# Gathering the rows of several experts in one product, behind a row norm applied before the split

## The chip, the core and the metric

The kernel runs on one core of a Trainium2 chip. The metric is the device time of one execution in microseconds (us). Engines are named as the profile names them: PE (TensorE, with PEld its weight loads), ACT (ScalarE), DVE (VectorE), POOL (GpSimd) and SP (SyncE, here the queue that issues the loads).

## What is computed

Two layers of a decoder trunk over 256 tokens of 1024 features, all in float32. Layer 0 has differential attention and a state-space scan, then a dense SwiGLU. Layer 1 has two other attention kinds, then a routed mixture of experts, with which this change deals:

```python
def rms_norm(t, gain):
    return t * rsqrt(mean(t * t, axis=-1) + 1e-6) * gain

def swiglu(h, w_gate, w_up, w_down):
    return (silu(h @ w_gate) * (h @ w_up)) @ w_down

h = rms_norm(x, od_norm_ffn)
logits = h @ router                           # 256 x 8
top_val, top_idx = top_k(logits, 2)
gates = sum(one_hot(top_idx, 8) * softmax(top_val)[..., None], axis=1)
for e in range(8):                            # w_gate, w_up: 1024 x 2816
    out = out + gates[:, e:e + 1] * swiglu(h, w_gate[e], w_up[e], w_down[e])
x = x + out
```

Each expert's three matrices are 34.6 MB together, and all eight are read in every execution.

## The kernel before

**Precision.** Products that need float32 are made of three faster ones: a value is split into a high and a low part (`wh` on ACT, `wl` on DVE for weights, `fh`/`fl` or `xnh`/`xnl` for rows), and `mm3` (L496 to L500) multiplies high by high, low by high and high by low.

**Routing** (L1305 to L1358). In two halves of 128 tokens the rows `x3` are transposed, multiplied by the router (products of 8 columns), and split unnormed into `xnh` and `xnl`; the row scale `rows` (`block_rstd`, L560) is worked out after the choice `m`. Products on `m` count the positions of the tokens in each expert. The experts are put in the order of their number of tokens; `ids` holds that order. The first four are the large ones (up to 128 tokens each), the last four the small ones (up to 64).

**Gathering.** An expert's tokens are brought together by a product with a one-hot matrix (`one_hots` L1415, `gather` L1427): for each of 8 blocks of 128 features four products, `xnh` and `xnl` by two halves of tokens. A pass takes the large expert of number p (128 columns) and its small partner (64 columns) at once, 192 columns; large rows are split on the way out, small ones copied to `xs`. Since the gathered rows aren't normed, `slot_scale` (L1440) gathers the row scales as well (products of one column), and Silu and the product of gate and up take them as operands. The first large expert is gathered before the loop (128 columns), its small partner in chunks 0 to 2 of that expert (64 columns), and each next pair in chunks 3 to 10 of the large expert before, one block of features in each.

**The loop.** An expert's 2816 inner features are 11 chunks of 256. A chunk of any expert needs three loads of 1 MiB: two of gate and up, one of down. A large chunk splits its weights and uses three products; a small chunk streams the raw weights by its rows. The order is fixed: LAG = 3 large chunks alone, then pairs of one large and one small chunk, then 3 small chunks alone. The down product of a chunk is put behind the gate and up products of the next one. Behind the last chunk of an expert its rows are scattered back by another one-hot product.

**The loads** all go through SP's queue in the order in which they are used (`Stream`, L673). A load needs a place: RAW = 4 raw buffers, and buffers of the earlier layers that have become free (`xres`, `xg0` up to unit XG = 12, `xg1`, `more`, `fl`). The addresses of all experts but the first two in line depend on `ids`, so SP reads `ids` (L1539) ahead of the first such load. Until the loop begins, work is recorded and ordered by a list scheduler (its lines are L312, DMAs L428); in the loop instructions stand as written (L317, DMAs L424).

If an expert had more than 128 tokens, a branch behind the loop would do its work in another way; it isn't taken here.

Of the kernel before, what the change touches and what calls it, by code (L numbers as in the profile page):

```python
# [19 lines left out]
P = 128  # L20
# [37 lines left out]
EXPLN = "natural_log_exp_and_others"  # L58
SILU = "silu_and_others"
# [316 lines left out]
def kernel(ctx: ExitStack, tc: tile.TileContext, a, out: bass.AP):  # L376
# [133 lines left out]
    def bc(ap, shape):  # L510
        return ap.to_broadcast(shape)
# [243 lines left out]
    def ff_act(gu, scales, act=None):  # L755
        hs = []
        for b in range(len(gu)):
            si = tw(256)
            (act or tact)(si, gu[b][:, 0:256], AF.Silu, scale=scales[b])
            hh = tw(256)  # L760
            V.scalar_tensor_tensor(hh, gu[b][:, 256:512], scales[b], si, op0=OP.mult, op1=OP.mult)
            hs.append(hh)
        return hs

# [553 lines left out]
    rows, slots = mo([P, 2], "rows"), mo([P, 8], "slots")  # L1318
# [93 lines left out]
    def one_hot(t, pos):  # L1412
        V.tensor_scalar(t, iota, pos, None, op0=OP.is_equal)

    def one_hots(p):  # L1415

        t = tw(dt=F32R).rearrange("p (b e s) -> p b e s", b=2, e=2)
        for b in range(2):
            one_hot(t[:, b, 0, :], (poso if p else posm)[:, b, p:p + 1])
            V.tensor_scalar(t[:, b, 1, :].rearrange("p (i s) -> p i s", i=2), bc(iota[:, None, 0:HALFP], [P, 2, HALFP]),  # L1420
                            poso[:, b, BIG + p:BIG + p + 1], None, op0=OP.is_equal)
        return t

    oh = {0: one_hots(0)}


    def gather(k, ohs, xb=None, xs=None):  # L1427

        lo, hi = 0 if xb else P, P + HALFP if xs is not None else P
        o = pa()[:, lo:hi]  # L1430
        for i, src in enumerate((xnh, xnl)):
            for b in range(2):
                mmx(o, src[:, b, k * P:(k + 1) * P], ohs(b)[:, lo:hi], i + b == 0, i + b == 2)
        gain = k2("gf1k", k, k + 1)
        if xb:
            split_gain(xb[0][:, k], xb[1][:, k], o[:, 0:P], gain)
        if xs is not None:
            S.activation(xs[:, k], o[:, P - lo:hi - lo], AF.Copy, scale=gain)

    def slot_scale(dst, ohs):  # L1440

        sp, n = pa(), ohs.shape[2]
        for e in range(n):
            for b in range(2):
                mmx(sp[:, e:e + 1], ohs[:, b, e, :].bitcast(F32), rows[:, b:b + 1], b == 0, b == 1)
        V.tensor_copy(dst, sp[:, 0:n])

    def oht_of(oh0, oh1):
        tp = pa()
# [24 lines left out]
                    dma(ov[:, b, cs], acc[:, b, cs])  # L1474
        rec.late = 0

    def large_tile(p):
        t = mo([P, 2, 8, P], "xg0", F32R) if p % 2 else gtile([P, 2, 8, P], F32R, "fh")
        return t[:, 0], t[:, 1]

    def small_tile():
        return rec.tile(mo.pool, [P, 8, HALFP], F32, "mxs", 2, name="xs")


    def sm_gu(xs, gu, u):
# [6 lines left out]
                    wv[:, :, i * P:(i + 1) * P], k == 0, k == 7)  # L1492
        st.done()

    def sm_act(gu, scale):
        si, hh = tw(P), tw(P)
        tact(si, gu[:, 0:P], AF.Silu, scale=scale)
        V.scalar_tensor_tensor(hh, gu[:, P:256], scale, si, op0=OP.mult, op1=OP.mult)
        return hh

    def sm_tr(hh):
# [49 lines left out]
    xb, xs = {0: large_tile(0)}, {}  # L1551
    for k in range(8):
        gather(k, lambda b: oh[0][:, b].rearrange("p e s -> p (e s)"), xb[0])
    rec.late = AFTER
    slot_scale(slots[:, 0:2], oh[0])
    rec.late = 0
    rec.flush([x3, oh[0], *xb[0], *st.tiles()])
    rec.on = False
    at.close()
    ov = out.rearrange("(b p) d -> p b d", p=P)  # L1560
    ys, ohts, hs, pend = {}, {}, {}, None
    N = len(items)
    for i in range(N + 1):
# [3 lines left out]
        if it:  # L1567
            sm, p, c = it
            gu = pa()
            xsp = [(xb[p][0], xb[p][1])] if not sm else xs[p]  # L1570
            sm_gu(xsp, gu, 0) if sm else ff_gu(st, xsp, [gu], 0, False)
        if was:
            t = sm_tr(hs[was]) if was[0] else ff_tr(hs[was])
        st.ahead(HL if alone or it[0] else HL - 1)
        if it:
            sm_gu(xsp, gu, 1) if sm else ff_gu(st, xsp, [gu], 1, False)
            e = 2 * p + sm
            hs[it] = sm_act(gu, slots[:, e:e + 1]) if sm else ff_act([gu], [slots[:, e:e + 1]])
        if alone or it[0]:
            st.ahead(HL)  # L1580
        if was:
# [12 lines left out]
        if not it:  # L1594
            continue
        if c == 1:
            ohts[sm] = oht_of(*(oh[p][:, b, int(sm), :] for b in range(2)))
        if sm:
            continue
        both = lambda b, q: oh[q][:, b].rearrange("p e s -> p (e s)")  # L1600
# [12 lines left out]
    scatter(*pend)  # L1613
    man.close()

# [2 lines left out]
    with tc.If(many > P):  # L1618
        with tc.For_i(0, 8, 1) as ei:
            col = small([P, 2, 2], "col")  # L1620
            V.tensor_copy(col[:, 0, :], posx[:, :, bass.ds(ei, 1)].rearrange("p b e -> p (b e)"))
            V.tensor_copy(col[:, 1, :], gate[:, :, bass.ds(ei, 1)].rearrange("p b e -> p (b e)"))
            ohx = tw(256, dt=F32R).rearrange("p (b s) -> p b s", b=2)
            for b in range(2):
                one_hot(ohx[:, b, :], col[:, 0, b:b + 1])
            xo = large_tile(1)
            for k in range(8):
                gather(k, lambda b: ohx[:, b, :], xo)
            slot_scale(slots[:, 0:1], ohx[:, :, None, :])
            to = oht_of(ohx[:, 0, :], ohx[:, 1, :])  # L1630
            yo = [[pa(), pa()]]
            st = Stream([a["moe"][bass.ds(ei * (3 * FC) + j, 1)].rearrange("u p c -> p (u c)") for j in range(3 * FC)])
            for c in range(FC):
                gu = [pa()]
                ff_gu(st, [xo], gu, 0)
                ff_gu(st, [xo], gu, 1)
                ff_dn(st, ff_tr(ff_act(gu, [slots[:, 0:1]], S.activation)), yo, c == 0, c == FC - 1)
            scatter(to, y_split(yo[0]), lambda b: col[:, 1, b:b + 1], x3)
        dma(ov, x3)
    mo.close()  # L1640


# [151 lines left out]
```

## Time and profile before

| what | value |
|---|---|
| median of 3 runs | 1177.9 us (1177.27 to 1180.31) |
| profiled execution | 1181.26 us, span 1179.5 us |
| PE busy | 1152.2 us, 98% of the span |
| PEld, DVE, ACT busy | 843.8, 718.6, 602.6 us |
| loaded from HBM | 345.95 MB, mean 294 GB/s over the span |
| share of PE in the chain that ended last | 83% (DMA 8%, DVE 4%, ACT 3%) |

The chain that ended last is followed back from the last instruction to whatever released each one. The expert loop runs from about 486 us to the end; before it lie the two layers' attention and the dense SwiGLU. In the windows below, a stretch of time is cut out of the span and each engine's busy time in it is given with its number of instructions. The timeline rows give start and length of one group of like instructions; a length reaches to the end of the last one, so neighbours overlap, and the distance of two starts tells what one took.

### The profile page before, as it was taken

The page shows a single profiled execution, that of the slowest core. Times are in us where ns is not written, and L with a number is a line of the kernel's source. Part 1 is how long each engine was busy: PE and PEld are TensorE (multiplying, and loading weights), DVE is VectorE, ACT ScalarE, POOL GpSimd, SP SyncE. Part 2 cuts the span into 40 slices and gives each one's busy share as a digit, 9 for nine tenths or more (in the row PEclk, how much of TensorE's full clock was granted, in tenths as well). Part 3 has the DMA queues.
Part 4 walks back from the last instruction along what each step waited for, and adds up shares of the span by engine and source line. Part 5 has one row for each costly group of instructions (what it writes and reads, how often), then busy time and mean ns, then how long its engine had stood idle before and what let it go on. Part 6 is the DMA issues. An engine that isn't in the chain of part 4 may idle for free.

```text
span 1179.5 us, 16563 instructions
## 1 busy us (share of the span) xinstructions
PE 1152.2 (98%) x6171; PEld 843.8 (72%) x6171; DVE 718.6 (61%) x1179; ACT 602.6 (51%) x1015; POOL 28.6 (2%) x59
## 2 busy tenths in 40 slices
PE   6999999999999999999999999999999999999997
PEld 6887888888777878876666666666666666666663
DVE  5999945444389765784555665556565546565542
ACT  5767743444388565564445444445445554444431
POOL 1040000000300000000000000000000000000000
PEclk9999999999999999799999999999999999999999
DMA  9443455556353513378999999999999999999994
GB/s 353 153 177 108 144 213 179 181 181 225 107 175 131 208 55 134 134 291 356 387 393 417 399 411 394 405 423 421 380 415 411 408 395 402 418 409 422 416 413 164
DMA packets 52069, 348.13 MB, mean 295 GB/s; under 512 B 5904, under 2 KB 6032, under 8 KB 11536
## 3 DMA queue, kind: packets, MB, share of 16 engines
q1 hardware_dynamic: 51984, 347.02, 74.6%
q8 instruction: 50, 0.82, 0.3%
q14 instruction: 35, 0.29, 0.1%
HBM read 345.95 MB, written 1.05 MB: 294 GB/s over the span
## 4 chain that ended last, share of the span: by engine, by line
PE 83%; DMA 8%; DVE 4%; ACT 3%; issue 2%; SPq 0%; DVEq 0%; ACTq 0%
PE ps L317 21%; PE ps L498 17%; PE ps L500 17%; PE ps L499 17%; PE ps L312 11%; DMA raw<-in_moe_dram 3%; ACT wh L317 2%; DVE wl L317 2%; DMA fl<-in_moe_dram 2%; DMA xg<-in_moe_dram 1%; DMA more<-in_moe_dram 1%; ACT tw L312 1%; DMA raw<-in_w_dram 1%; DMA xres<-in_moe_dram 1%; DVE wl L312 0%
## 5 line engine op out<-in xcount | busy, mean ns | idle before, releaser
L317 DVE TENSOR_TENSOR wl<-raw,wh 128x2048 fp32r<-128x2048 f32 x90 | 206.3, 2293 | 160.7 <-ACT wh L317 160.7
L317 ACT ACTIVATE wh<-raw 128x2048 fp32r<-128x2048 f32 x90 | 172.0, 1911 | 118.1 <-DMA raw<-in_moe_dram 63.9
L498 PE MATMUL ps<-wh,fh 128*128 128x512 f32 (+2 forms) x544 | 221.5, 407 | 0.0
L499 PE MATMUL ps<-wl,fh 128*128 128x512 f32 (+2 forms) x544 | 211.3, 388 | 0.0
L500 PE MATMUL ps<-wh,fl 128*128 128x512 f32 (+2 forms) x368 | 142.2, 387 | 0.0
L317 ACT ACTIVATE tw<-ps 128x128 f32<-128x128 f32 (+2 forms) x114 | 43.3, 388 | 180.0 <-PE ps L317 178.0
L498 PEld LDWEIGHTS ps<-wh,fh 128*128 128x128 f32 x544 | 103.2, 190 | 20.6 <-ACT tw L312 0.3
L498 PE MATMUL ps<-wh,tw 128*128 128x512 f32 (+1 forms) x276 | 113.9, 413 | 1.7 <-ACT tw L317 1.0
L499 PEld LDWEIGHTS ps<-wl,fh 128*128 128x128 f32 x544 | 103.1, 190 | 17.3
L500 PE MATMUL ps<-wh,tw 128*128 128x512 f32 (+1 forms) x276 | 109.0, 395 | 0.0
L499 PE MATMUL ps<-wl,tw 128*128 128x512 f32 (+1 forms) x276 | 108.9, 395 | 0.0
L312 DVE TENSOR_TENSOR wl<-raw,wh 128x512 fp32r<-128x512 f32 (+1 forms) x149 | 98.9, 679 | 2.9 <-ACT wh L312 2.8
L317 DVE TENSOR_TENSOR tw<-ps,tw 128x256 fp32r<-128x256 f32 (+1 forms) x70 | 35.9, 521 | 91.8 <-ACT tw L317 91.6
L312 ACT ACTIVATE wh<-raw 128x512 fp32r<-128x512 f32 (+1 forms) x135 | 77.7, 623 | 19.7 <-PE ps L500 16.1
L317 PE MATMUL ps<-raw,xs 128*64 128x256 f32 x720 | 87.2, 384 | 0.0
L500 PEld LDWEIGHTS ps<-wh,fl 128*128 128x128 f32 x368 | 69.1, 188 | 14.8 <-DVE fl L312 0.7
L498 PEld LDWEIGHTS ps<-wh,tw 128*128 128x128 f32 x276 | 51.8, 188 | 28.1 <-issue 15.4
L498 PE MATMUL ps<-wh,xg 128*128 128x512 f32 x176 | 71.0, 403 | 0.0
L500 PE MATMUL ps<-wh,fh 128*128 128x512 f32 x176 | 69.8, 396 | 0.0
L317 PEld LDWEIGHTS ps<-raw,xs 128*64 128x64 f32 x720 | 48.4, 136 | 29.8 <-issue 8.5
L500 PE MATMUL ps<-wh,xg 128*128 128x512 f32 x176 | 69.3, 394 | 0.0
L499 PE MATMUL ps<-wl,xg 128*128 128x512 f32 x176 | 68.7, 390 | 0.0
(295 smaller groups left out, 1807.3 us busy)
## 6 DMA issues: line engine op xcount, KB each, us to landing
raw<-in_moe_dram SPq DMA_DIRECT2D x131, 1024.0 KB, 9.3
xg<-in_moe_dram SPq DMA_DIRECT2D x33, 1024.0 KB, 8.9
xres<-in_moe_dram SPq DMA_DIRECT2D x33, 1024.0 KB, 8.3
more<-in_moe_dram SPq DMA_DIRECT2D x32, 1024.0 KB, 8.7
fl<-in_moe_dram SPq DMA_DIRECT2D x32, 1024.0 KB, 8.6
raw<-in_ffn_dram SPq DMA_DIRECT2D x30, 1024.0 KB, 4.8
raw<-in_w_dram SPq DMA_DIRECT2D x23, 1024.0 KB, 5.2
raw<-in_ffn_dram SPq DMA_DIRECT2D x12, 256.0 KB, 3.8
```

Of the source, the lines that this page charges most:

```text
L312: return (self.name, self.cost(fn, args, kw), lambda: real(*args, **kw))
L317: return getattr(self.eng, fn)(*args, **kw)
L498: nc.tensor.matmul(ps, xh, wh, start=start, stop=False)
L499: nc.tensor.matmul(ps, xh, wl, start=False, stop=False)
L500: nc.tensor.matmul(ps, xl, wh, start=False, stop=stop)
```

## The change

- The row scale is worked out ahead of the split, and `split_gain` puts it into `xnh` and `xnl`. The gathered rows are normed, `slot_scale` and `slots` go, and Silu and the product of gate and up lose their scale operands.
- `one_hots(lo, n, width)` makes one-hot matrices of several experts. All four small experts are gathered in one pass (4 x 64 columns) in chunks 0 to 3 of the first large expert, two blocks of features in each. Large experts 1 and 2 are gathered together (2 x 128 columns) in chunks 6 to 9 of the first, and large expert 3 (128 columns) in chunks 2 to 5 of the second. ACT copies them unsplit to a tile in the place `xg0`.
- `large_split` splits an expert's rows into the one tile `fh` behind the gate and up products of the last chunk of the expert before it (one ACT copy, one DVE subtraction, 128x1024).
- RAW 4 to 5, XG 12 to 14, LAG 3 to 4.
- `WARM` = 8 products of 512 columns, whose result is not used, stand between the router products and the products on `m`.

```diff
-RAW = 4
+RAW = 5
...
-XG = 12
+XG = 14
...
-LAG = 3
+LAG = 4
+WARM = 8
...
+            if scales:
...
+            else:
+                (act or tact)(si, gu[b][:, 0:256], AF.Silu)
+                V.tensor_tensor(hh, gu[b][:, 256:512], si, OP.mult)
...
         rx3 = rows[:, b:b + 1]
+        block_rstd(x3, b, rx3)
...
-            flex(xnh[:, b, cs], x3[:, b, cs])
-            V.tensor_tensor(xnl[:, b, cs], x3[:, b, cs], xnh[:, b, cs].bitcast(F32), OP.subtract)
+            split_gain(xnh[:, b, cs], xnl[:, b, cs], x3[:, b, cs], rx3)
...
-        block_rstd(x3, b, rx3)
...
+    idle = pa()
+    rec.late = AFTER
+    for i in range(WARM):
+        mmx(idle, u3r[:, 0:P], xnh[:, 1, 0:512], True, True)
+    rec.late = 0
...
+    def one_hots(lo, n, width=P):
+
+        t = tw(2 * n * width, dt=F32R).rearrange("p (b e s) -> p b e s", b=2, e=n)
         for b in range(2):
...
+            V.tensor_tensor(t[:, b], bc(iota[:, None, 0:width], [P, n, width]),
+                            bc(poso[:, b, lo:lo + n, None], [P, n, width]), OP.is_equal)
         return t
...
+    def gather_all(k, oh, dst):
+
+        n, w = oh.shape[2], oh.shape[3]
+        o, gain = gather(k, lambda b: oh[:, b].rearrange("p e s -> p (e s)"), n * w)
+        S.activation(dst[:, :, k], o.rearrange("p (e s) -> p e s", e=n), AF.Copy, scale=gain)
...
+    def large_split(src):
+        x = large_tile()
+        S.activation(x[0], src, AF.Copy)
+        V.tensor_tensor(x[1], src, x[0].bitcast(F32), OP.subtract)
+        return x
...
-    slot_scale(slots[:, 0:2], oh[0])
...
+            if not sm and c == FC - 1 and p < BIG - 1:
+                xb = large_split(xl[:, p % 2])
...
         if p == 0 and c < LAG:
-            if c == 0:
-                xs[0] = small_tile()
-            for k in range(c * 3, min(8, c * 3 + 3)):
-                gather(k, lambda b: both(b, 0), None, xs[0])
-        if p < BIG - 1 and c == 2:
-            oh[p + 1] = one_hots(p + 1)
-        if p < BIG - 1 and c >= LAG:
-            if c == LAG:
-                xb[p + 1], xs[p + 1] = large_tile(p + 1), small_tile()
-                slot_scale(slots[:, 2 * p + 2:2 * p + 4], oh[p + 1])
-            gather(c - LAG, lambda b: both(b, p + 1), xb[p + 1], xs[p + 1])
+            for k in range(2 * c, 2 * c + 2):
+                gather_all(k, oh_s, xs)
+        if p == 0 and LAG + 2 <= c < LAG + 6:
+            if c == LAG + 2:
+                xl, oh_l = mo([P, 2, 8, P], "xg0"), one_hots(1, 2)
+            for k in range(2 * (c - LAG - 2), 2 * (c - LAG - 1)):
+                gather_all(k, oh_l, xl)
+        if p == 1 and 2 <= c < 6:
+            if c == 2:
+                oh_l = one_hots(3, 1)
+            for k in range(2 * c - 4, 2 * c - 2):
+                gather_all(k, oh_l, xl[:, 0:1])
```

On PE, between the router products (`tw` 128x8) and the first gather products (`tw,xnh` 128x128), before:

```order
L312 MATMUL ps<-cp,xres 128x128 x16
L312 MATMUL ps<-tw 128x8 x16
L312 MATMUL ps<-m,tw 128x8
L312 MATMUL ps<-m,tw 128x16
L312 MATMUL ps<-m,tw 128x8 x2
L312 MATMUL ps<-tw,xnh 128x128 x5
```

and after (`xnh,tw` 128x512 are the spare products):

```order
L313 MATMUL ps<-cp,xres 128x128 x4
L313 MATMUL ps<-tw 128x8 x12
L313 MATMUL ps<-xnh,tw 128x512 x8
L313 MATMUL ps<-m,tw 128x8
L313 MATMUL ps<-m,tw 128x16
L313 MATMUL ps<-m,tw 128x8 x2
L313 MATMUL ps<-tw,xnh 128x128 x5
```

The eight spare products stand where PE had nothing between the last router product and the first on `m`.

On SP, the expert loads ahead of the reading of `ids`, before:

```order
L428 DMA xg_3349<-in_moe_dram 128x2048
L428 DMA raw<-in_moe_dram 128x2048 x4
L428 DMA xres<-in_moe_dram 128x2048
L428 DMA raw<-in_moe_dram 128x2048 x2
L428 DMA xg_3356<-in_moe_dram 128x2048
L428 DMA more<-in_moe_dram 128x2048
L428 DMA fl<-in_moe_dram 128x2048
L1539 TENSOR_LOAD ids
```

and after:

```order
L429 DMA raw<-in_moe_dram 128x2048
L429 DMA xg_3350<-in_moe_dram 128x2048
L429 DMA raw<-in_moe_dram 128x2048 x4
L429 DMA xres<-in_moe_dram 128x2048
L429 DMA raw<-in_moe_dram 128x2048 x2
L429 DMA xg_3357<-in_moe_dram 128x2048
L429 DMA more<-in_moe_dram 128x2048
L429 DMA fl<-in_moe_dram 128x2048
L429 DMA raw<-in_moe_dram 128x2048 x2
L1558 TENSOR_LOAD ids
```

Eleven loads stand ahead of `ids` before, fourteen after.

On PE, chunk 3 of the third large expert with the small chunk behind it, before:

```order
L500 MATMUL ps<-wh,fh 128x512
L317 MATMUL ps<-fl,tw 64x512 x4
L317 MATMUL ps<-rows,tw 128x1 x4
L317 MATMUL ps<-tw,xnh 128x192 x2
L317 MATMUL ps<-tw,xnl 128x192 x2
L317 MATMUL ps<-xg_7522,xs 64x256 x8
L317 MATMUL ps<-cp,tw 128x128 x2
L317 MATMUL ps<-raw,xs 64x256 x8
```

and after:

```order
L501 MATMUL ps<-wh,fh 128x512
L318 MATMUL ps<-more,tw 64x512 x4
L318 MATMUL ps<-fl,xs 64x256 x8
L318 MATMUL ps<-cp,tw 128x128 x2
L318 MATMUL ps<-raw,xs 64x256 x8
```

The slot products (128x1) and gather products (128x192) are gone from this chunk.

## Rows read from the trace of the kernel before

**Rows 1.** The page: busy time of engines, and the clock's slices
```profile
PE 1152.2 (98%) x6171; PEld 843.8 (72%) x6171; DVE 718.6 (61%) x1179; ACT 602.6 (51%) x1015; POOL 28.6 (2%) x59
...
PEclk9999999999999999799999999999999999999999
```

**Rows 2.** Windows: start:end length, busy PE PEld DVE ACT POOL, clock, DMA share, GB/s
```profile
689.11:859.91 170.80, 170.80 (x932) 113.59 (x930) 99.31 (x93) 83.01 (x97) 0.00 (x0) 1.00 0.99 406
859.91:1030.75 170.84, 170.84 (x931) 113.51 (x930) 98.15 (x89) 83.81 (x98) 0.00 (x0) 1.00 0.99 407
```

**Rows 3.** Windows of single pairs, the first with a gather, the others without
```profile
722.53:737.76 15.23, 15.23 (x85) 10.07 (x84) 7.93 (x9) 7.59 (x9) 0.00 (x0) 1.00 1.01 424
...
1062.31:1076.78 14.47, 14.47 (x82) 9.65 (x80) 7.40 (x7) 6.84 (x7) 0.00 (x0) 1.00 1.01 423
...
1105.69:1121.39 15.70, 14.51 (x81) 9.64 (x80) 7.95 (x6) 7.02 (x8) 0.00 (x0) 1.00 1.01 421
1121.39:1136.28 14.89, 14.53 (x81) 9.63 (x80) 7.96 (x6) 6.57 (x7) 0.00 (x0) 1.00 1.00 398
```

**Rows 4.** Timeline of PE around one gather: start, length, line, operation, shapes, count
```profile
727.34 0.47 PE L317 MATMUL ps<-tw,xnh 128*128 128x192 f32 x2
...
727.96 1.95 PE L317 MATMUL ps<-raw,xs 128*64 128x256 f32 x16
```

**Rows 5.** Timeline of PE at narrow products; groups from 486 us on (busy, mean ns)
```profile
493.65 0.30 PE L317 MATMUL ps<-tw,xnh 128*128 128x64 f32 x2
...
494.90 0.48 PE L498 MATMUL ps<-wh,fh 128*128 128x512 f32 x1
...
363.89 0.28 PE L498 MATMUL ps<-wh,tw 128*128 128x256 f32 x1
...
364.60 0.40 PE L498 MATMUL ps<-wh,fh 128*128 128x512 f32 x1
...
L317 PE MATMUL ps<-tw,xnh 128*128 128x192 f32 x48 | 11.1, 314 | 0.0
...
L317 PE MATMUL ps<-rows,tw 128*128 128x1 f32 x24 | 3.1, 248 | 0.0
```

**Rows 6.** The routing stretch: its window, then timeline of PE and of DVE
```profile
473.21:490.28 17.07, 14.48 (x59) 13.46 (x59) 13.13 (x73) 6.18 (x15) 0.00 (x0) 0.50 0.33 112
...
469.98 4.08 PE L312 MATMUL ps<-tw 128*128 128x8 f32 x32
475.83 1.02 PE L312 MATMUL ps<-m,tw 128*128 128x8 f32 x4 [1.78 <-DVE m L312]
477.66 1.30 PE L312 MATMUL ps<-tw,xnh 128*128 128x128 f32 x5 [0.81 <-DVE rank L312]
...
484.52 1.81 PE L312 MATMUL ps<-rows,tw 128*128 128x1 f32 x8
486.19 0.77 PE L498 MATMUL ps<-wh,fh 128*128 128x512 f32 x1
...
490.18 0.45 PE L498 MATMUL ps<-wh,fh 128*128 128x512 f32 x1
...
478.23 0.68 DVE L312 TENSOR_TENSOR wl<-raw,wh 128x512 fp32r<-128x512 f32 x1
```

**Rows 7.** Waits (total, times, longest) of ACT, SP, PE; timeline of ACT; page's groups
```profile
ACT wh L317 <- DMA raw<-in_moe_dram: 63.9, 24, 5.4
...
SPq L1539 <- DVE ids L312: 11.9, 1, 11.9
...
PE ps L317 <- DVE tw L317: 2.8, 6, 1.2
...
1106.30 1.91 ACT L317 ACTIVATE wh<-more 128x2048 fp32r<-128x2048 f32 x1 [5.57 <-DMA more<-in_moe_dram]
...
L317 DVE TENSOR_TENSOR wl<-raw,wh 128x2048 fp32r<-128x2048 f32 x90 | 206.3, 2293 | 160.7 <-ACT wh L317 160.7
L317 ACT ACTIVATE wh<-raw 128x2048 fp32r<-128x2048 f32 x90 | 172.0, 1911 | 118.1 <-DMA raw<-in_moe_dram 63.9
```

More of the change, by code (lines that the diff above doesn't have):

```diff
@@ L753, in ff_gu, with ff_act @@
                     wl[:, kk * 512:(kk + 1) * 512], k == 0, k == 7)
-    def ff_act(gu, scales, act=None):
+    def ff_act(gu, scales=None, act=None):
         hs = []
@@ L758, in ff_act @@
             si = tw(256)
-            (act or tact)(si, gu[b][:, 0:256], AF.Silu, scale=scales[b])
             hh = tw(256)
-            V.scalar_tensor_tensor(hh, gu[b][:, 256:512], scales[b], si, op0=OP.mult, op1=OP.mult)
+            if scales:
+                tact(si, gu[b][:, 0:256], AF.Silu, scale=scales[b])
+                V.scalar_tensor_tensor(hh, gu[b][:, 256:512], scales[b], si, op0=OP.mult, op1=OP.mult)
+            else:
+                (act or tact)(si, gu[b][:, 0:256], AF.Silu)
+                V.tensor_tensor(hh, gu[b][:, 256:512], si, OP.mult)
             hs.append(hh)
@@ L1317 @@
     ids = mo([P, 8], "ids", I32)
-    rows, slots = mo([P, 2], "rows"), mo([P, 8], "slots")
+    rows = mo([P, 2], "rows")
     for b in range(2):
         rx3 = rows[:, b:b + 1]
+        block_rstd(x3, b, rx3)
         lps = pa()
@@ L1424, with both_halves @@
[L1424 to L1430, printed above, removed]
+            V.tensor_tensor(t[:, b], bc(iota[:, None, 0:width], [P, n, width]),
+                            bc(poso[:, b, lo:lo + n, None], [P, n, width]), OP.is_equal)
+        return t
+    def both_halves(r):
+        t = tw(256, dt=F32R).rearrange("p (b s) -> p b s", b=2)
+        for b in range(2):
+            V.tensor_scalar(t[:, b].rearrange("p (i s) -> p i s", i=2), bc(iota[:, None, 0:HALFP], [P, 2, HALFP]),
+                            poso[:, b, r:r + 1], None, op0=OP.is_equal)
+        return t
@@ L1431, in gather @@
+    oh0 = tw(256, dt=F32R).rearrange("p (b s) -> p b s", b=2)
+    for b in range(2):
+        one_hot(oh0[:, b], posm[:, b, 0:1])
+    def gather(k, ohs, n):
+        o = pa()[:, 0:n]
         for i, src in enumerate((xnh, xnl)):
             for b in range(2):
[L1433 to L1446, printed above, removed]
+                mmx(o, src[:, b, k * P:(k + 1) * P], ohs(b), i + b == 0, i + b == 2)
+        return o, k2("gf1k", k, k + 1)
+    def gather_split(k, ohs, x):
+        o, gain = gather(k, ohs, P)
+        split_gain(x[0][:, k], x[1][:, k], o, gain)
@@ L1493, in sm_gu, with sm_act @@
         st.done()
-    def sm_act(gu, scale):
+    def sm_act(gu):
         si, hh = tw(P), tw(P)
-        tact(si, gu[:, 0:P], AF.Silu, scale=scale)
-        V.scalar_tensor_tensor(hh, gu[:, P:256], scale, si, op0=OP.mult, op1=OP.mult)
+        tact(si, gu[:, 0:P], AF.Silu)
+        V.tensor_tensor(hh, gu[:, P:256], si, OP.mult)
         return hh
@@ L1550 @@
                        [(place("xg1"), 999), (place("more"), 999), (place("fl"), 999)]), whole)
-    xb, xs = {0: large_tile(0)}, {}
+    xb = large_tile()
     for k in range(8):
-        gather(k, lambda b: oh[0][:, b].rearrange("p e s -> p (e s)"), xb[0])
-    rec.late = AFTER
-    slot_scale(slots[:, 0:2], oh[0])
-    rec.late = 0
-    rec.flush([x3, oh[0], *xb[0], *st.tiles()])
+        gather_split(k, lambda b: oh0[:, b], xb)
+    rec.flush([x3, *xb, *st.tiles()])
     rec.on = False
     at.close()
+    top = scope("t")
+    xs = top([P, BIG, 8, HALFP], "xs")
+    oh_s = one_hots(BIG, BIG, HALFP)
     ov = out.rearrange("(b p) d -> p b d", p=P)
@@ L1569 @@
             gu = pa()
-            xsp = [(xb[p][0], xb[p][1])] if not sm else xs[p]
+            xsp = xs[:, p] if sm else [xb]
             sm_gu(xsp, gu, 0) if sm else ff_gu(st, xsp, [gu], 0, False)
@@ L1576 @@
             sm_gu(xsp, gu, 1) if sm else ff_gu(st, xsp, [gu], 1, False)
-            e = 2 * p + sm
-            hs[it] = sm_act(gu, slots[:, e:e + 1]) if sm else ff_act([gu], [slots[:, e:e + 1]])
+            hs[it] = sm_act(gu) if sm else ff_act([gu])
+            if not sm and c == FC - 1 and p < BIG - 1:
+                xb = large_split(xl[:, p % 2])
         if alone or it[0]:
@@ L1596 @@
         if c == 1:
-            ohts[sm] = oht_of(*(oh[p][:, b, int(sm), :] for b in range(2)))
+            o = both_halves(BIG + p) if sm else one_hots(p, 1)[:, :, 0]
+            ohts[sm] = oht_of(o[:, 0], o[:, 1])
         if sm:
             continue
-        both = lambda b, q: oh[q][:, b].rearrange("p e s -> p (e s)")
         if p == 0 and c < LAG:
-            if c == 0:
-                xs[0] = small_tile()
-            for k in range(c * 3, min(8, c * 3 + 3)):
-                gather(k, lambda b: both(b, 0), None, xs[0])
-        if p < BIG - 1 and c == 2:
-            oh[p + 1] = one_hots(p + 1)
-        if p < BIG - 1 and c >= LAG:
-            if c == LAG:
-                xb[p + 1], xs[p + 1] = large_tile(p + 1), small_tile()
-                slot_scale(slots[:, 2 * p + 2:2 * p + 4], oh[p + 1])
-            gather(c - LAG, lambda b: both(b, p + 1), xb[p + 1], xs[p + 1])
+            for k in range(2 * c, 2 * c + 2):
[10 more added lines that the diff above has]
+                gather_all(k, oh_l, xl[:, 0:1])
     scatter(*pend)
@@ L1625 @@
                 one_hot(ohx[:, b, :], col[:, 0, b:b + 1])
-            xo = large_tile(1)
+            xo = large_tile()
             for k in range(8):
-                gather(k, lambda b: ohx[:, b, :], xo)
-            slot_scale(slots[:, 0:1], ohx[:, :, None, :])
+                gather_split(k, lambda b: ohx[:, b, :], xo)
             to = oht_of(ohx[:, 0, :], ohx[:, 1, :])
@@ L1636 @@
                 ff_gu(st, [xo], gu, 1)
-                ff_dn(st, ff_tr(ff_act(gu, [slots[:, 0:1]], S.activation)), yo, c == 0, c == FC - 1)
+                ff_dn(st, ff_tr(ff_act(gu, None, S.activation)), yo, c == 0, c == FC - 1)
             scatter(to, y_split(yo[0]), lambda b: col[:, 1, b:b + 1], x3)
         dma(ov, x3)
+    top.close()
     mo.close()
```

11 lines of the change are left out of this document (2 added, 9 removed).

## The prediction

> **What bounds the kernel now.** I read the page's busy times and slices first, then windows cut at the same point of each expert's cycle, then single pairs of chunks, then the routing stretch. The reader is to see four things.
>
> TensorE (PE) is busy 1152.2 of 1179.5 us, and the clock line shows one slice below nine tenths [rows 1]. In the expert loop the middle two cycles (from chunk 3 of one large expert to chunk 3 of the next) are 170.80 and 170.84 us, with PE busy for all of it [rows 2]. So there only work taken off PE can shorten the span.
>
> Second, the same windows show DMA shares of 0.99 at 406 and 407 GB/s, and pairs that run at 423 to 424 GB/s [rows 2, 3]. 424 is the most that any of these rows shows. One unit is 1.049 MB, 2.48 us at 423 GB/s; a pair of chunks (one large, one small) needs six, 14.88 us. A pair without gathers takes 14.47 us on PE, one with gathers 15.23 us [rows 3]. The loads are nearly as long as the products: a cycle's 66 units are 163.7 us at that pace, which is where this change would bring PE (below).
>
> Third, ACT stands 63.9 us for loads into raw places [rows 7], yet PE's largest group of waits between 490 and 1172 us is 2.8 us for DVE's tw, six times [rows 7]. The bottleneck is PE with about one pair of slack, not the loads.
>
> Fourth, at routing the granted clock is 0.50 over 17.07 us [rows 6], the lower of the two levels, 1.2 instead of 2.4 GHz, and PE waits 1.78 and 0.81 us for DVE there [rows 6].
>
> **The gathers (the main term).** Before, expert 0's small partner takes 32 products of 64 columns; twelve such fill 493.65 to 494.90, 0.104 us each [rows 5], so 3.3 us. Then 24 pairs (eight in each of three cycles; the counted group has 48 of the hi kind in 24 pairs [rows 5]) each take four products of 192 columns. What a gather costs there is the pair difference, 15.23 − 14.47 = 0.76 us [rows 3]: in the timeline its four products fill 727.34 to 727.96 [rows 4] and the rest shows at the next product. 24 × 0.76 = 18.2 us. The slot products in the loop are 24, 3.1 us [rows 5]. Together 24.6 us.
>
> After, three sets of 32 products remain: the four small experts (256 columns, eight in each of chunks 0 to 3, no pair yet), large experts 1 and 2 (256 columns, four chunks), expert 3 (128 columns, four chunks). Products of 256 columns follow each other at 0.118 us (363.89 to 364.60, six) [rows 5]; 128 lies between 64 and 256 columns, 0.108. To this comes an edge: a pair's 0.76 less four products at some 0.113 is 0.31 us for each place where gathers interrupt the stream. An estimate: 12 × (8 × 0.118 + 0.31) less 4 × 8 × 0.01 for the narrower ones = 14.7 us. Lower bound without any edge 11.0; upper bound with every product at 0.76/4 = 0.19 us, 18.2. The saving is 24.6 − 14.7 = **9.9 us**, between 6.4 and 13.6, all of it on an engine that is fully busy there.
>
> The sum of columns is the same before and after (20,480), and so the Trainium skill has a rule against this term: "TensorE: Matmul & The Clock Gate", section "Back-to-back issue gap", gives N/2.4 + 2.5 ns for an isolated product at full clock. By it the regrouping saves 32 gaps of 2.5 ns, 0.08 us, and what is left of the term is the slot products. The rows contradict it at the narrow end: 64 columns take 0.104 us and 256 take 0.118 [rows 5], so width is nearly free there; the same page's section "LDWEIGHTS" (columns of the weights by 1.2, 107 ns for 128) fits those rows.
>
> **Routing and the front.** Removed: eight slot products, 484.52 to 486.19, 1.67 us at half clock [rows 6]. Added: eight spare products of 512 columns that stand ahead of the first product on m, at about 0.44 us each there (nine products as wide start between 486.19 and 490.18 [rows 6]), 3.5 us. Their cover: PE is idle 1.78 us before that product [rows 6], and m comes later, because the row scale (a Square on ACT, small DVE operations) is now ahead of the split, and the second half's 512-wide splits on DVE (0.68 us each [rows 6]) carry the gain. I count three such operations more before m, 2.0 us. So the idle place is 3.8 us and the spare products fit; without that cover they would cost up to 3.5. The path pays DVE's 2.0 less 1.67: **+0.3 us** if the clock stays as it is. If the clock is up when the first large expert's 32 gather products begin, these (477.66 to 484.52, 6.9 us [rows 6]) take 32 × 0.108 = 3.5, and the nine wide products up to 490.18 take half their 4.0: 3.4 and 2.0 us gone, −5.1 us in all with the +0.3. What rows show of the clock: it came back at 490.2, after 12.5 us in which PE worked almost without a stop from 477.66 [rows 6]; the spare products start that work 3 us earlier at least, with wide products. I take **−2.0**, bounds −5.1 and +2.0 (more DVE work than counted).
>
> **Splitting the unsplit rows.** Three times, at the last chunk of a large expert, ACT copies 128x1024 and DVE subtracts. Half of the 2048-wide rows is 0.96 and 1.15 us [rows 7]. Next use is the next expert's first chunk; between lie a small chunk's products and the down products of two chunks, two thirds of a pair, some 9 us. Hidden, unless ACT stands at a load for more than 6 us just then; the longest seen is 5.57 [rows 7]. The old per-chunk evacuations with their splits (24 on ACT and 24 on DVE) go. The scale operands of Silu and product disappear at no cost. Taken at 0, bounds 0 and +3 × 1.2 (the longest wait of PE there [rows 7]).
>
> **Fifth raw place, three more loads early, LAG 4.** SP has eleven expert loads ahead of the first load whose address needs `ids`, and stands 11.9 us for it [rows 7]; after, fourteen. One place more is 2.48 us more lead. With LAG 4 there are 40 pairs instead of 41, and one large and one small chunk more alone; PE's products are the same. What waits of PE there are (2.8 us the largest group [rows 7]) may go; new ones may come, since PE is faster while the loads aren't. **+0.5**, bounds −2.8 and +6.6 (rival A).
>
> **Sum.** −9.9 − 2.0 + 0 + 0.5 = −11.4 us: 1181.3 (the profiled execution; span 1179.5) becomes 1169.9. The median of the runs is 3.4 us under the profiled one, so the forecast is **1166.5 us**, of itself between 1162 and 1171.
>
> **Rivals.**
> *A, the loads become the bound.* Sixteen pairs lose their gathers. If each runs at the loads' 14.88 instead of 14.47 us, 16 × 0.41 = 6.6 us are given back: about 1173. For it: DMA share 1.01 in these pairs [rows 3], and the two last gather-free pairs of the trace stretch to 15.70 and 14.89 [rows 3]. Against it: over a whole cycle PE after is 170.80 − 8 × 0.76 − 1.0 = 163.7 us, which equals 66 loads, and each expert's change gives the loads time, which the places can carry over.
> [...]
> *B, slower.* The mechanism: ACT is first in, first out. When a load is late, ACT stands at its split (5.57 us at 1106.30 [rows 7]), the evacuation queued behind it is late, PE waits (up to 1.2 us [rows 7]), places free late, and SP issues the next load late. In before the gathers give time back; without them the state could last. The two pairs in which the trace shows it take 15.70 and 14.89, 15.30 in the mean [rows 3]. A cycle has 4.6 us beside its pairs (170.80 − 8 × 15.23 − 3 × 14.47 less 1.0 of slots), so it would be 11 × 15.30 + 4.6 = 172.9, and the 3.6 cycles 7.6 us longer than now; with the front's −2.0 it is 1183.5. It is slower from a mean pair of about 15.1 us upward. Against it: the gather-free pair from 1062.31 ran at PE's pace, with PE busy for all of it [rows 3].
> *C, everything lands.* No edge in the gathers, full clock by the first gathers, no waits: −13.6 − 5.1 + 0 would be 1159.
> *D, the change doesn't do what it says:* wide products cost in proportion to their columns, only slots and the front are saved, −3.1 − 2.0 + 0.5: 1173.3.
>
> **How the numbers follow.** Forecast 0.58; A 0.16; B 0.07; C 0.11; D 0.04; a mixture of small losses (A with a longer DVE path in front, 1175 to 1180) 0.04. The range is from 1159.5 to 1175.5: below it most of C, above it B and part of A and of the mixture. A measurement of this kernel can tell about 0.3%, 3.5 us, from no change; under 1174.4 count the forecast, C, D and three quarters of A: 0.85. Within: 0.25 of A and the mixture, 0.08. Slower: 0.07.
>
> **What would show it.** Expert cycles of 164 us instead of 170.8, with PE still busy for all of it, would confirm the gathers; cycles near 168 with PE idle and ACT's waits on loads doubled would be A; pairs of over 15.1 us without gathers B. Three groups of 32 gather products at about 0.12 us each decide the main term. In front, the granted clock in the 17 us after routing and the time from the last router product to the first expert product (474.06 to 486.19 now [rows 6]) decide the second. I'd be wrong altogether if the gathers' cost is the edge alone and each edge grows with the products in it.

## The result, and the profile after

The changed kernel takes 1190.61 us (median of 4 runs, 1189.10 to 1192.02) against 1177.88 before: 1.0094 times as long, with an interval of 1.0079 to 1.0108. It is slower, where 1166.5 us were forecast, and outside the range of 1159.5 to 1175.5. The profiled execution has a span of 1190.2 us, 10.7 more than before. In a run further below (early one-hots, places as before) one of eight executions took 2865.79 us where the others took 1171.42 to 1179.93; it is left out of that run's median, and its cause isn't known.

The page of the changed kernel, the lines that answer to [rows 1]:

```profile
PE 1150.0 (97%) x6115; PEld 843.7 (71%) x6115; DVE 711.5 (60%) x1162; ACT 591.1 (50%) x986; POOL 28.7 (2%) x59
...
PEclk9999999999999999789999999999999999999999
```

PE has 56 products fewer, and is busy for only 2.2 us less, in a span that is 10.7 us longer. So the time went into waiting and into products that take longer. PE's waits from the first expert product on (total, times, longest), which answer to the last kind of row in [rows 7]:

```profile
PE ps L318 <- DVE tw L318: 17.3, 11, 4.5
```

2.8 us have become 17.3. The single pairs, in windows with the columns of [rows 3], first two with gather products (two blocks of large experts 1 and 2, then of expert 3), then one without, show PE busy for all of their length, so the gathers are not the cause:

```profile
601.92:617.65 15.73, 15.73 (x89) 10.56 (x88) 7.74 (x6) 7.56 (x9) 0.00 (x0) 1.00 1.00 387
696.18:711.81 15.63, 15.63 (x89) 10.52 (x88) 7.74 (x6) 7.35 (x9) 0.00 (x0) 1.00 1.01 411
...
776.69:791.13 14.44, 14.44 (x82) 9.65 (x80) 7.40 (x7) 6.73 (x7) 0.00 (x0) 1.00 1.01 424
```

Pairs without gathers follow each other at 14.44 us with PE busy throughout. What is late lies at chunk 1 of the first large expert and of each small one. The timeline of PE there, for the second small expert, and then of DVE over the same stretch:

```profile
741.93 0.39 PE L501 MATMUL ps<-wh,tw 128*128 128x512 f32 x1
744.75 0.43 PE L318 MATMUL ps<-cp,tw 128*128 128x128 f32 x2 [2.42 <-DVE tw L318]
744.94 0.47 PE L499 MATMUL ps<-wh,fh 128*128 128x512 f32 x1
```

```profile
739.71 2.29 DVE L318 TENSOR_TENSOR wl<-more,wh 128x2048 fp32r<-128x2048 f32 x1 [1.38 <-ACT wh L318]
741.92 0.28 DVE L318 TENSOR_TENSOR tw<-ps,tw 128x128 f32<-128x128 f32 x1
742.12 2.28 DVE L318 TENSOR_TENSOR wl<-xres,wh 128x2048 fp32r<-128x2048 f32 x1
744.32 0.47 DVE L318 TENSOR_SCALAR tw<-c,poso 128x128 fp32r<-128x128 f32 x2
```

The two products `cp,tw` at 744.75 are the transposes of the one-hots with which the expert's rows will be scattered back ten chunks later (`oht_of`). They need the two operations `tw<-c,poso`, 0.47 us of work that depend on nothing but the routing. But these stand in DVE's queue behind the weight split of a 2048-wide unit (2.28 us from 742.12), and start only as that ends, at 744.32; PE, whose next products stand behind the transposes, does nothing for 2.42 us. Before the change there was no such operation in this place: the one-hots had been made for the gather, during the expert before, and `oht_of` took the same tile. With the gathers regrouped that tile is gone, and a new one is made where it is needed. The diff printed ahead of the prediction leaves these lines of the change out:

```diff
         if c == 1:
-            ohts[sm] = oht_of(*(oh[p][:, b, int(sm), :] for b in range(2)))
+            o = both_halves(BIG + p) if sm else one_hots(p, 1)[:, :, 0]
+            ohts[sm] = oht_of(o[:, 0], o[:, 1])
```

In the first large expert the same wait is 4.53 us; the other small experts have 2.32, 2.58 (at 911.74) and 2.70 us. These five are 14.6 of the 17.3 us; the other large experts' one-hots stand behind less in DVE's queue, at 0.5 us each. Three of the five in PE's timeline:

```profile
509.39 0.69 PE L318 MATMUL ps<-cp,tw 128*128 128x128 f32 x2 [4.53 <-DVE tw L318]
...
564.88 0.53 PE L318 MATMUL ps<-cp,tw 128*128 128x128 f32 x2 [2.32 <-DVE tw L318]
...
1078.95 0.69 PE L318 MATMUL ps<-cp,tw 128*128 128x128 f32 x2 [2.70 <-DVE tw L318]
```

Behind some of these waits the products themselves are slow. Windows of the stretches right behind the five:

```profile
509.40:516.10 6.70, 6.70 (x24) 5.69 (x25) 0.56 (x2) 0.95 (x2) 0.00 (x0) 0.57 0.60 243
564.90:569.50 4.60, 4.60 (x15) 3.48 (x16) 0.55 (x2) 0.00 (x0) 0.00 (x0) 0.65 1.01 427
744.80:747.80 3.00, 3.00 (x15) 2.44 (x16) 0.42 (x1) 0.00 (x0) 0.00 (x0) 1.00 1.02 421
912.00:915.00 3.00, 3.00 (x16) 2.45 (x16) 0.42 (x1) 0.00 (x0) 0.00 (x0) 1.00 1.02 429
1079.00:1083.20 4.20, 4.20 (x14) 3.42 (x15) 0.52 (x2) 0.00 (x0) 0.00 (x0) 0.68 1.03 431
```

Behind the waits of 4.53, 2.32 and 2.70 us the granted clock fell to 1.2 GHz for part of the window (mean 0.57, 0.65 and 0.68); behind those of 2.42 and 2.58 us it stayed up. The three windows would be shorter by 6.70 x 0.43 + 4.60 x 0.35 + 4.20 x 0.32 = 5.8 us at full clock (an estimate). With the waits, 17.3 − 2.8 = 14.5, that is 20.3 us (an estimate, for its second part) that the change added and that stand in no term of the prediction.

### The profile page after: what moved, and what is told of

It reads as the page before. It is cut to its first block, busy times and chain, and to the rows that moved or that the text cites. A ratio compares the mean times of both kernels' runs of the same rounds, so it can differ in the third digit from the quotient of the medians.

```text
span 1190.2 us, 16408 instructions
## 1 busy us (share of the span) xinstructions
PE 1150.0 (97%) x6115; PEld 843.7 (71%) x6115; DVE 711.5 (60%) x1162; ACT 591.1 (50%) x986; POOL 28.7 (2%) x59
## 4 chain that ended last, share of the span: by engine, by line
PE 73%; DMA 13%; DVE 6%; ACT 6%; issue 2%; SPq 0%; ACTq 0%; DVEq 0%
PE ps L318 17%; PE ps L499 16%; PE ps L501 15%; PE ps L500 15%; DMA xres<-in_moe_dram 13%; PE ps L313 11%; DVE wl L318 4%; ACT wh L318 4%; ACT tw L313 1%; DMA raw<-in_w_dram 1%; ACT wh L313 0%; DVE tw L318 0%; DVE wl L313 0%; ACT xg L313 0%; DVE tw L313 0%
## 5 line engine op out<-in xcount | busy, mean ns | idle before, releaser
L499 PE MATMUL ps<-wh,fh 128*128 128x512 f32 (+2 forms) x720 | 293.7, 408 | 0.0
L500 PE MATMUL ps<-wl,fh 128*128 128x512 f32 (+2 forms) x720 | 281.7, 391 | 0.0
L318 ACT ACTIVATE tw<-ps 128x128 f32<-128x128 f32 (+2 forms) x202 | 72.8, 363 | 366.8 <-PE ps L318 334.1
L499 PEld LDWEIGHTS ps<-wh,fh 128*128 128x128 f32 x720 | 137.6, 191 | 29.2 <-issue 0.5
L318 DVE TENSOR_TENSOR tw<-ps,tw 128x256 f32<-128x256 f32 (+3 forms) x158 | 66.6, 427 | 150.0 <-ACT tw L318 149.8
L500 PEld LDWEIGHTS ps<-wl,fh 128*128 128x128 f32 x720 | 137.2, 191 | 23.9
L501 PE MATMUL ps<-wh,fh 128*128 128x512 f32 x352 | 139.9, 397 | 0.0
L318 PE MATMUL ps<-raw,xs 128*64 128x256 f32 x960 | 116.3, 384 | 0.0
L318 DVE TENSOR_TENSOR wl<-xres,wh 128x2048 fp32r<-128x2048 f32 x39 | 89.2, 2287 | 19.8 <-ACT wh L318 19.5
L318 ACT ACTIVATE wh<-xres 128x2048 fp32r<-128x2048 f32 x39 | 74.9, 1919 | 27.9 <-DMA xres<-in_moe_dram 27.8
L501 PEld LDWEIGHTS ps<-wh,fh 128*128 128x128 f32 x352 | 67.4, 191 | 14.9
```

The lines of the kernel that those rows point to most:

```text
L318: return getattr(self.eng, fn)(*args, **kw)
L499: nc.tensor.matmul(ps, xh, wh, start=start, stop=False)
L500: nc.tensor.matmul(ps, xh, wl, start=False, stop=False)
L501: nc.tensor.matmul(ps, xl, wh, start=False, stop=stop)
```

## Experiments

Two theories stood against each other. Theory 1: the late one-hots are the whole loss. Theory 2: the loads hold PE back (rival A or B of the prediction), and the one-hots are only where PE meets it. For theory 2 spoke that 13% of the chain that ended last was loads into `xres`, and that splits ahead of the one-hots wait for ACT (1.38 us at 739.71).

Beside the medians I give each profiled execution's length from the first expert product to the end of its span, since the time up to it varies: in the five kernels that share the changed kernel's front (but for the places of loads) it lies between 484.5 and 488.3 us. From there on it takes 693.3 us before (486.19 to 1179.5), 701.9 after (488.29 to 1190.2).

**One-hots a chunk earlier.** In the changed kernel:

```diff
+        if c == 0:
+            pre[sm] = both_halves(BIG + p) if sm else one_hots(p, 1)[:, :, 0]
         if c == 1:
-            o = both_halves(BIG + p) if sm else one_hots(p, 1)[:, :, 0]
+            o = pre[sm]
             ohts[sm] = oht_of(o[:, 0], o[:, 1])
```

> The changed kernel with one edit: the one-hot matrices of the scatter are made at an expert's chunk 0 instead of chunk 1, so that DVE has them long before PE transposes them. Theory 1 (late one-hots: DVE makes them behind the weight splits of chunk 1, PE waits 17.3 us in 11 waits, and works some 5 us longer at half clock after the three longest): 15 to 22 us less than the changed kernel, 1169 to 1176 us, no PE wait over 1 us on tw in the loop. Theory 2 (the loads hold PE back, and the waits only show where PE meets them): the waits turn up at other places and the time stays within 4 us of 1190.6.

Measured: 1167.62 us, 0.9891 of before (0.9872 to 0.9909), 23.0 us less than the changed kernel; 679.5 us from the first expert product on. PE's waits in the loop, then DVE's making of the second small expert's one-hots and PE's transposes of them:

```profile
PE ps L318 <- DVE tw L318: 1.3, 3, 0.6
```

```profile
716.11 0.47 DVE L318 TENSOR_SCALAR tw<-c,poso 128x128 fp32r<-128x128 f32 x2
```

```profile
728.57 0.40 PE L501 MATMUL ps<-wh,tw 128*128 128x512 f32 x1
728.81 0.38 PE L318 MATMUL ps<-cp,tw 128*128 128x128 f32 x2
728.94 0.47 PE L499 MATMUL ps<-wh,fh 128*128 128x512 f32 x1
```

The same operations, the same lengths, 12 us ahead of their use: no wait. Theory 1 is borne out; the gain is 1 us more than its 15 to 22. Theory 2 would have left the time within 4 us of 1190.6. With this edit the change takes about what was forecast for it (1166.5).

**The same fault put into the kernel before.** Nothing of the change but one-hots made anew at chunk 1:

```diff
-            ohts[sm] = oht_of(*(oh[p][:, b, int(sm), :] for b in range(2)))
+            o = tw(256, dt=F32R).rearrange("p (b s) -> p b s", b=2)
+            for b in range(2):
+                if sm:
+                    V.tensor_scalar(o[:, b].rearrange("p (i s) -> p i s", i=2), bc(iota[:, None, 0:HALFP], [P, 2, HALFP]),
+                                    poso[:, b, BIG + p:BIG + p + 1], None, op0=OP.is_equal)
+                else:
+                    V.tensor_tensor(o[:, b], iota, bc(poso[:, b, p:p + 1], [P, P]), OP.is_equal)
+            ohts[sm] = oht_of(o[:, 0], o[:, 1])
```

> The kernel before with one edit: at chunk 1 of every expert the one-hots for the scatter are made anew on DVE, just ahead of their transposes, instead of taking those that the gather already had. Nothing else of the change. Theory 1: 10 to 20 us slower than before, 1188 to 1198 us, with PE waits of 2 to 5 us on DVE's tw at the large experts' chunk 1. Theory 2 (loads): 16 small DVE operations more, under 2 us, 1178 to 1180.

Measured: 1209.11 us, 1.0250 of before (1.0231 to 1.0268), 29.7 us slower than its own runs of before. That is more than the 10 to 20 us that I expected, and the long waits are at chunk 1 of the first large expert (4.62 us) and of the last three small ones (2.84 to 4.22), not of all large ones. PE's waits, and the one-hots of the second small expert on DVE and PE:

```profile
PE ps L317 <- DVE tw L317: 20.7, 10, 4.6
```

```profile
730.80 0.34 DVE L317 SCALAR_TENSOR_TENSOR tw<-ps,slots,tw 128x128 f32<-128x128 f32 x1
732.80 2.29 DVE L317 TENSOR_TENSOR wl<-raw,wh 128x2048 fp32r<-128x2048 f32 x1 [1.66 <-ACT wh L317]
735.01 0.48 DVE L317 TENSOR_SCALAR tw<-c,poso 128x128 fp32r<-128x128 f32 x2
```

```profile
735.43 0.43 PE L317 MATMUL ps<-cp,tw 128*128 128x128 f32 x2 [4.22 <-DVE tw L317]
```

Here the wait is 4.22 us, since the split ahead has itself stood 1.66 us for ACT: the wait is the split's 2.3 us and whatever that split waits for. Sixteen operations with 3.8 us of work cost nearly 30: the waits grew from 2.8 to 20.7 us, and the mean granted clock over the span fell from 0.990 to 0.981, by an estimate (0.019 x 1207.6 less 0.010 x 1179.5) another 11 us.

**Only the transposes later.** DVE's queue left as the change made it, PE's transposes moved from chunk 1 to chunk 2:

```diff
         if c == 1:
-            o = both_halves(BIG + p) if sm else one_hots(p, 1)[:, :, 0]
+            pre[sm] = both_halves(BIG + p) if sm else one_hots(p, 1)[:, :, 0]
+        if c == 2:
+            o = pre[sm]
             ohts[sm] = oht_of(o[:, 0], o[:, 1])
```

> The changed kernel with the scatter's one-hots made at chunk 1 as there, and only their transposes on PE moved one chunk back, to chunk 2. DVE's queue stays as it is. Theory 1 (PE meets one-hots that are still behind splits in DVE's queue): as e1_early, 1165 to 1171 us, no wait over 1 us. If the place of the one-hots in DVE's own queue costs (later splits, later loads): part of the 23 us stays, 1175 us or more.

Measured: 1167.56 us (1166.30 to 1168.84), 679.9 us from the first expert product on, and no wait over 0.8 us. The place in DVE's queue costs nothing; that PE asks too early does. Either end can be moved.

**Places as before**, first in the changed kernel, then in the one with early one-hots:

```diff
-RAW = 5
+RAW = 4
...
-XG = 14
+XG = 12
```

> The changed kernel with RAW 4 and XG 12, as before, in place of 5 and 14. Theory 1: at most 3 us either way, the waits for one-hots stay. Theory 2 (loads hold PE back): with a place less in the loop 5 us slower or more, with PE waits in the gather-free pairs, which now run at 14.44 us.

Measured: 1203.88 us, 1.0209 of before (1.0189 to 1.0229), 13.3 us more than the changed kernel; PE's waits and one of the chains, the last small expert's, first on ACT, then DVE, then PE:

```profile
PE ps L318 <- DVE tw L318: 24.2, 14, 5.1
```

```profile
1081.71 1.91 ACT L318 ACTIVATE wh<-raw 128x2048 fp32r<-128x2048 f32 x1 [3.10 <-DMA raw<-in_moe_dram]
```

```profile
1083.65 2.29 DVE L318 TENSOR_TENSOR wl<-raw,wh 128x2048 fp32r<-128x2048 f32 x1 [2.69 <-ACT wh L318]
1085.86 0.48 DVE L318 TENSOR_SCALAR tw<-c,poso 128x128 fp32r<-128x128 f32 x2
```

```profile
1086.20 0.69 PE L318 MATMUL ps<-cp,tw 128*128 128x128 f32 x2 [5.10 <-DVE tw L318]
```

ACT stands 3.10 us for a load, DVE 2.69 us for ACT, the one-hots stand behind DVE's split, and PE stands for the one-hots. My expectation from theory 1, at most 3 us either way, missed: the loads lengthen the wait, and so theory 2 has a part. Whether they cost without it, the second run tells.

> The changed kernel with the scatter's one-hots at chunk 0 (as in e1_early, 1167.6) and with RAW 4 and XG 12 as before. With late one-hots the places were worth 13 us (1203.9 against 1190.6). If they were only worth that because a late load lengthened the wait for the one-hots (DVE has the split of that load in its queue ahead of them): within 3 us of 1167.6 here. If the load lead counts by itself: 5 us or more slower.

Measured: 1173.5 us (1171.42 to 1179.93), 0.9961 of before (0.9940 to 0.9981), against 1167.62 and 0.9891 with five places: about 6 us slower, and 684.8 us from the first expert product on against 679.5. That is my second case: the load lead counts by itself. The waits of PE, and of ACT for loads (the largest group from 640 to 1130 us), in this kernel:

```profile
PE ps L318 <- DVE tw L318: 6.1, 9, 1.2
```

```profile
ACT wh L318 <- DMA raw<-in_moe_dram: 61.2, 23, 5.6
```

In the kernel with early one-hots and five places ACT's waits for loads into raw places in the same stretch are 0.4 us, and those for loads into all places 46.4 against 120.0 us here. Most pairs without gathers still take 14.44 us with the places as before; in six PE waits 0.2 to 1.2 us for DVE's `tw` (4.8 us together) behind splits that came late (at 889.74 PE waits 1.14 us; the split of 881.83 had stood 4.39 us for ACT, and ACT 4.80 us for a load). So the two settings of the places together are worth some 6 us by themselves once the gathers are out of the pairs, and 13 when a late load also delays the one-hots. RAW and XG were not tried apart.

**Without the spare products**, in the changed kernel and in the one with early one-hots:

```diff
-    idle = pa()
-    rec.late = AFTER
-    for i in range(WARM):
-        mmx(idle, u3r[:, 0:P], xnh[:, 1, 0:512], True, True)
-    rec.late = 0
```

> The changed kernel without the eight spare products. Theory 1 and 2 alike say nothing of it. If the spare products are hidden (they end at 479.87 us, m is there at 479.95) and do nothing for the clock: within 1 us of 1190.6. If they bring the clock back earlier: 1 to 3 us slower. If they stand in the way: up to 3.6 us faster.

Measured: 1192.42 us (1189.23 to 1193.73): by the medians 1.8 us slower, as in the second case, but not to be told from 1190.61 (1189.10 to 1192.02).

> e1_early without the eight spare products. They lie where PE waits for DVE's m, and the clock came back at 491.2 us in the changed kernel and at 490.3 in the one before, so they bring nothing: within 1.5 us of 1167.6. If they give the clock back earlier: 1.5 to 4 us slower.

Measured: 1168.92 us (1168.10 to 1169.87) against 1167.62 (1165.68 to 1167.88): 1.3 us slower, and the runs don't overlap; but the intervals of the two kernels relative to their own runs of before do (0.9893 to 0.9931 and 0.9872 to 0.9909), so the difference isn't clear. In windows from 473 to 492 us the granted clock is 0.55 and 0.64 with the spare products (changed kernel, early one-hots):

```profile
473.00:492.00 19.00, 18.02 (x70) 16.06 (x71) 15.26 (x77) 6.97 (x17) 0.00 (x0) 0.55 0.37 137
```

```profile
473.00:492.00 19.00, 17.97 (x76) 15.62 (x77) 14.94 (x75) 7.40 (x18) 0.00 (x0) 0.64 0.40 144
```

and 0.50 and 0.51 without. They are hidden, and may bring back the worth of a microsecond of the clock (not shown), not the five that would have come with a full clock at the first gather product.

**The split behind the choice.** The kernel with early one-hots and without spare products, with the split moved:

```diff
-            split_gain(xnh[:, b, cs], xnl[:, b, cs], x3[:, b, cs], rx3)
...
         V.tensor_tensor(m[:, b, :], s1, s2, OP.add)
+        for i in range(2):
+            cs = slice(i * 512, (i + 1) * 512)
+            split_gain(xnh[:, b, cs], xnl[:, b, cs], x3[:, b, cs], rx3)
```

> e6_early_nowarm with the normed split recorded behind the choice m, so that DVE makes m before the second half's splits where it can. In the changed kernel m came at 479.9 us against 475.9 before. If the order of DVE's queue there is what delays m: 1 to 3 us faster than e6_early_nowarm. If the row scale's chain or the router products set m: within 1 us.

Measured: 1169.09 us, no difference to 1168.92. But the edit did not do what it was meant to do: the list scheduler put the two operations that make `xnl` into the same place again, between the second half's logits (`lg`) and the choice m. DVE in this kernel:

```profile
476.79 0.17 DVE L313 COPY lg<-ps 128x8 f32<-128x8 f32 x1 [0.20 <-PE ps L313]
476.88 0.74 DVE L313 SCALAR_TENSOR_TENSOR xnl<-xres,rows,xnh 128x512 fp32r<-128x512 f32 x1
477.53 0.16 DVE L313 MAX8 t<-lg 128x8 f32<-128x8 f32 x1
477.61 0.73 DVE L313 SCALAR_TENSOR_TENSOR xnl<-xres,rows,xnh 128x512 fp32r<-128x512 f32 x1
...
479.82 0.16 DVE L313 TENSOR_TENSOR m<-sel,sel 128x8 fp32r<-128x8 f32 x1
```

So this run doesn't settle what makes m late, and no run here moves the splits out of the way. The traces of before and after part the 4.0 us by which m comes later (475.98 and 479.95). The copy of the logits behind the last router product starts 2.3 us later (474.14 and 476.43). From there to m it takes 1.8 us before and 3.5 us after, 1.7 us more, and in that stretch after, not before, stand these two operations with 0.74 and 0.75 us. Of the 2.3 us, PE's waits for ACT's `tw` (0.40 and 0.47 us, none before) are a part; the rest is left open.

**LAG 3, and what came with it.** In the kernel with early one-hots:

```diff
-LAG = 4
+LAG = 3
...
-            for k in range(2 * c, 2 * c + 2):
+            for k in range(3 * c, min(8, 3 * c + 3)):
                 gather_all(k, oh_s, xs)
```

> e1_early with LAG 3 instead of 4: one pair more, one large and one small chunk alone less, the small experts' rows in three chunks. PE's products are the same, so within 2 us of 1167.6 if PE is the bound; 3 to 7 us slower if the loads need the fourth chunk's lead (a pair takes 14.44 us on PE, its six loads 14.88 at 423 GB/s).

Measured: 1165.93 us (1165.14 to 1166.56), 1.7 us under 1167.62; relative to before, 0.9887 and 0.9891 can't be told apart. In the profiled executions two things work against each other: the first expert product comes at 481.4 us instead of 486.5, and from there it takes 682.5 us instead of 679.5. The list scheduler, which plans the recorded stretch, takes another one of its four settings here, and that orders the work before the experts differently. Why LAG changes its choice is not shown.

With LAG 4 again and the setting fixed in the recorder:

```diff
-        for alpha, *way, late, after in self.WAYS:
+        self.flushes = getattr(self, "flushes", 0) + 1
+        for alpha, *way, late, after in self.WAYS[2:3] if self.flushes == 2 else self.WAYS:
```

> e1_early with one of the list scheduler's four settings fixed for the recorded stretch of the second layer: the one that the scheduler itself takes with LAG 3 (e7_early_lag3), LAG stays 4. In e7_early_lag3 the first expert product came at 481.4 us against 486.5 in e1_early, though LAG touches nothing ahead of it, and from there to the end it took 682.5 against 679.5 us. If the setting is the reason for the first, and LAG 3 for the second: 3 to 5 us faster than e1_early, 1163 to 1165 us. If LAG 3 gave the time: as e1_early, 1167.6.

Measured: 1163.40 us, 0.9867 of before (0.9850 to 0.9883), the fastest kernel here: first expert product at 483.4 us, 679.6 us from there, as expected. So the setting gives some 3 to 4 us (0.9867 against 0.9891 of before, 1163.40 against 1167.62 us; the intervals just overlap), and LAG 4, with its gathers in four chunks instead of three, about 3 (679.6 against 682.5 with the same setting; 1163.40 against 1165.93 us).

## Why the prediction was wrong

**What bounds the kernel** was read rightly: PE, with the loads near. With one-hots early, an expert's cycle from one `large_split` to the next (794.52 to 958.15) is 163.6 us with PE busy for all of it, where the prediction named 164 us as the sign. A stretch that begins in it and runs a little further, at 421 GB/s:

```profile
820.65:967.64 146.99, 146.99 (x804) 98.26 (x803) 82.20 (x70) 69.32 (x73) 0.00 (x0) 1.00 1.01 421
```

Pairs without gathers take 14.44 us there. Rival A, the loads as the bound, did not come in: the even stretch to 14.88 us is not seen.

**The step that failed** is the part on the gathers, where I counted what the regrouping takes off PE and adds to it, and not that the old one-hots had a second reader, the scatter. The sum has no term for making them anew; their cost was put at nothing without a reason. The change has it in one line at `c == 1`, which neither the diff ahead of the prediction nor the prediction names. For `large_split` the prediction asked when its result is next used and what may delay it; for these operations it did not. It cost 14.5 us of waits and, by estimate, 5.8 us of products at half clock by the trace, and 23.0 us by the experiment. Against the kernel with early one-hots the waits differ by 17.3 − 1.3 = 16.0 us, and with the 5.8 that is 21.8 of the 22.4 us by which the two differ from the first expert product on. Rival B had the right sign and a wrong mechanism for this loss: it took late loads with a queue behind ACT's splits as the cause, which at this place only lengthens the wait. What it describes shows by itself, in waits of up to 1.2 us, with the places as before.

**The gathers**: −9.9 us forecast (−6.4 to −13.6). Measured by one pair window of each kind: four pairs at 15.73 − 14.44 = 1.29 us, four at 15.63 − 14.44 = 1.19, and four times 0.95 in the first expert's chunks (495.20 to 496.15 for one), 13.7 us in all where 14.7 were taken; so −10.9. The rows

```profile
606.72 0.50 PE L318 MATMUL ps<-tw,xnh 128*128 128x256 f32 x2
607.06 0.40 PE L318 MATMUL ps<-tw,xnl 128*128 128x256 f32 x2
607.30 0.40 PE L318 MATMUL ps<-tw,xnh 128*128 128x256 f32 x2
607.53 0.40 PE L318 MATMUL ps<-tw,xnl 128*128 128x256 f32 x2
```

show products of 256 columns, behind the first two, at 0.118 us, as in [rows 5]. Rival D (cost by columns) falls.

**Routing and the front**: −2.0 forecast, +2.1 in the profiled execution of the changed kernel (488.3 against 486.2), +0.3 with early one-hots, where nothing of the front was edited; in the kernels that share this front the first expert product lies between 484.5 and 488.3 us, so that the term is not told from 0. That the spare products are hidden was right here (with the scheduler's other setting, in the last experiment, they are not quite: m is there at 474.55 us, and the products on m begin behind them at 474.92). The hoped-for part, a full clock at the gathers, came for part of them at most; the +0.3 of "the clock stays as it is" was the better term, and its inside was off. DVE's part was nearly right (1.7 us where 2.0 were counted), but the router products ended 2.3 us later, which was not counted: m came 4.0 us later, and the spare products ended just then, at 479.9.

**Splitting the unsplit rows** at no cost: right, with early one-hots PE's only waits in the loop are 0.6 and 0.5 us at the gathers, and 0.4 and 0.2 us at the end.

**Fifth raw place and LAG**: +0.5 forecast, between −2.8 for waits that go and +6.6 for rival A. With early one-hots the waits in the loop went and no new ones came, about −2.5. With the places as before some 5 us more are lost in the loop (684.8 against 679.5), in single waits, and with LAG 3 about 3.

**In sum**, without the late one-hots: 693.3 − 679.5 = 13.8 us off the loop (10.9 gathers and slots, 2.5 waits: 2.8 for DVE's `tw` and 1.0 for ACT's became 1.3; 0.4 open), and 0.3 more in front. In the profiled executions that is 1181.3 to 1167.8, where the prediction's sum led to 1169.9. That the medians, 1167.62 and the forecast 1166.5, lie so near is in part luck: the loop saved 4.4 us more than its terms (−9.9 + 0.5), the front 2.3 us less, and the profiled execution with early one-hots lies 0.2 us over its median, where 3.4 were taken off.

## What to carry to other kernels

When a change regroups work, look for every reader of what the old grouping left behind: a tile that was a by-product has to be made again, and the place where it is made is set by the code's order, not by when its inputs are there. Half a microsecond of work on an engine that works its queue in order, as DVE did here, costs what stands ahead of it in that queue; make such a thing a step ahead of its use, or use it a step later. An edit to a program that a scheduler orders should be looked up in the trace before its time is read. Compare kernels from a mark inside the program as well as by their total, since a planner may reorder a stretch that the edit never touched.

## What the runs showed of the hardware

Waits of PE of 2.3 to 4.5 us in a stretch of full clock were followed, in three of the five cases (4.53, 2.32 and 2.70 us), by a clock at the lower level for part of the next 4 to 7 us, and in two (2.42 and 2.58 us) not. Where the clock fell, the slower products cost by estimate another 1.3 to 2.9 us: 4.53 us of waiting and 2.9 us of slower products at 509.4.

Products of 256 columns, each with weights of its own, followed each other at 0.118 us at full clock. The Trainium skill, "TensorE: Matmul & The Clock Gate", section "Back-to-back issue gap", gives N/2.4 + 2.5 ns for an isolated product, 109 ns for 256 columns; the rows above have 118.
